# Hybrid attention and RWKV-7 block: block inverses made beside the chain of the unit ahead, q, k, v projections moved to the front

## The chip, the cores and the metric

The kernel runs on one core of a Trainium2 chip. The metric is device time in microseconds (us), the median of repeated executions. The engines are TensorE (PE in the rows, its weight loads PEld), VectorE (DVE), ScalarE (ACT), GpSimd (POOL) and SyncE (SP), which issues the DMAs.

## What is computed

One layer of a hybrid decoder block on 1024 positions of 1024 channels, in float32:

```python
u = rmsnorm(h, norm1_gain)
proj = u @ w_in
q, k, v, r_p, k_p, v_p, w_p, a_p, g_p, gate_a, gate_b = jnp.split(proj, split_at, axis=-1)
y_attn = sliding_window_attention(q, k, v, ...) @ w_branch_attn      # 8 blocks of 128 queries
y_rwkv = rwkv7_time_mix(r_p, k_p, v_p, w_p, a_p, g_p, ...) @ w_branch_rwkv
mixed = jax.nn.sigmoid(gate_a) * y_attn + jax.nn.sigmoid(gate_b) * y_rwkv
h = h + mixed @ w_out
hidden = jnp.square(jax.nn.relu(rmsnorm(h, norm2_gain) @ w_ff_in))
return h + hidden @ w_ff_out
```

The time mixing is a recurrence over positions, for each of 8 heads:

```python
def step(S, inp):
    r_t, w_t, k_t, v_t, a_t, b_t = inp
    sa = jnp.einsum('bhij,bhj->bhi', S, a_t)
    S = S * w_t[:, :, None, :] + sa[..., None] * b_t[:, :, None, :] + v_t[..., None] * k_t[:, :, None, :]
    return S, jnp.einsum('bhij,bhj->bhi', S, r_t)
```

## The kernel before

Every float32 matmul of the projections is made of three matmuls of split operands (a high and a low part), 128 by 128 weights by 512 columns. A projection of 128 output channels is 48 of them (`proj`, line 169, tile `ps_m`), or is part of a Strassen product (`group`, line 233, tile `psw`).

The program goes through these stages:

1. **Front.** The norm (`norm1`), two projections, then two branch gates (`gate`, tile `gt`). Meanwhile `in_sums` makes the seven right sides of the Strassen products, on DVE, ACT and POOL. `in_groups` then makes 16 of the projections in four groups (`GROUPS`), among them four gates.
2. **Phase 1.** The SBUF pools of the front are closed and others opened in their place, so phase 1 starts when the groups are through. It projects and prepares k, v and q (`prep_k`, `prep_v`, `prep_q`, `prep_rq`), and then works through eight *units*: one of four pairs of heads (p), one half of the sequence (hf). A unit has three parts:
   - `unit_e` (E): decays, keys and the 64 by 64 score blocks of the unit. Two pairs of score products `ps_s` (tag `s`, two buffers) are masked by DVE into `SA` and `SR` (line 673; two buffers of each). Parts of `SA` go to DRAM and come back as `LT`. Then DVE inverts 16 by 16 blocks in 15 steps of a product and a sum (lines 710 and 711), and the result goes out to `lx_d`.
   - `unit_m` (M): the inverse comes back as `XT`. From it PE, DVE and ACT make 64 by 64 inverses, in four rounds of small matmuls (`ps_z`, `ps_x`, with `ps_g` ahead of them; `XD` and `DZ` are DVE's transposes).
   - `unit_c` (C), *the chain*: eight chunks of 64 positions, one after the other. In each the state gives `ry` (PE), DVE adds it to `G0`, PE makes `pu`, DVE copies it to `UV` (line 788, eight in a chain), PE makes `pd`, and DVE the next state `sbd`. Behind the last chunk PE makes `py` from `UV` and `SR`, DVE adds it to `Yt`, normalises it, and writes `y` (line 830).
   
   Attention blocks (`attn_block`), the output gate of the time mixing (`prep_g`) and eight branch gates fill in by the table `PLAN`: one entry ahead of the units, one behind each unit.
3. **Branch stage.** Attention and time mixing are loaded as `yh`, `yl`, two last gates are made, then the branch projections, `w_out` and the MLP, as before and after alike.

A scheduler decides the order of each engine from priorities: `tc.high_priority(offset=...)` moves work forward by so many instructions (`HP_E` for E, `HP_C` for M and C). Each engine then works through its own list in order. A tile is taken when its buffer is free, so tags and buffer numbers also set the order. `M` and `C` share the tag `c` of PSUM (one buffer); `py` and the transposes behind it have the tag `y` (one buffer).

Of the kernel before, what the change touches and what calls it, by code (L numbers as in the profile page):

```python
# [60 lines left out]
def hybrid_block(ctx, tc, x_ap, xt_ap, win_ap, wst_ap, lora_ap, wbr_ap, wout_ap, wff1_ap, wff2_ap, cst_ap,  # L61
# [306 lines left out]
    wst = ExitStack()  # L368
    wp = wst.enter_context(tc.tile_pool(name="wspool", bufs=1))
    for i in range(2):  # L370
        gate(i)
    B_in = in_sums(wp)
    pqt.close()
    pw = [None, wst.enter_context(tc.tile_pool(name="pw1", bufs=1, space=PSUM, side="right"))]
    pst.close()
    pw[0] = wst.enter_context(tc.tile_pool(name="pw0", bufs=1, space=PSUM))
    pw.reverse()
    in_groups(wp, pw, B_in)
    wst.close()
    psum_pools(1)  # L380

# [5 lines left out]
    def phase1():  # L387
        st = ExitStack()
        lp = st.enter_context(tc.tile_pool(name="lpool", bufs=1))
        rp = st.enter_context(tc.tile_pool(name="rpool", bufs=1))  # L390
        ep = st.enter_context(tc.tile_pool(name="epool", bufs=1))
        ap = st.enter_context(tc.tile_pool(name="apool", bufs=1))

        cst[1] = lp.tile([P, CTOT - CKEEP], F32, name="cst1")
        nc.sync.dma_start(out=cst[1], in_=cst_ap[:, CKEEP:])
        smask = lp.tile([P, HALF], F32, name="smask")
        G.memset(smask, 1.0)
        G.memset(smask[:, ::64], 0.0)
# [15 lines left out]

        g0, g1, full = slice(0, 64), slice(64, 128), slice(0, 128)

        def prep_k():
            w = load_w(win_ap[2])
            for hf in range(2):
# [7 lines left out]
                rk = newton(ep, pk, 8, 1.0 / 64, RMS_EPS)  # L427
                rkx = ep.tile([P, 8, 64], F32, tag="e0", bufs=2, name="rkx")
# [23 lines left out]
        def prep_q(j):  # L452
            w = load_w(win_ap[4 + j])
            for hf in range(2):
# [4 lines left out]
                split_out(ps, [P, HALF], *(("k", "kkn") if hf else ("cum", "Wi")),  # L459
# [255 lines left out]
        def unit_m(p, hf, X):  # L715
            SA, UV, un = X["SA"], X["UV"], X["un"]
            G0 = rp.tile([P, 4, 128], F32, tag="G0", name="G0", bufs=1)
            half_ = [slice(0, 64), slice(64, 128)]
            ps = pp.tile([P, 4, 2, 64], F32, tag="c", name="ps_g", bufs=1)
# [17 lines left out]
            ps = pp.tile([P, 8, 64], F32, tag="c", name="ps_z", bufs=1)  # L737
# [4 lines left out]
            ps = pp.tile([P, 8, 64], F32, tag="c", name="ps_x", bufs=1)  # L742
# [10 lines left out]
            ps = pp.tile([P, 8, 32], F32, tag="c", name="ps_z", bufs=1)  # L753
# [5 lines left out]
            ps = pp.tile([P, 8, 32], F32, tag="c", name="ps_x", bufs=1)  # L759
# [87 lines left out]
        cnt = {"q": 0, "a": 0, "x": 6}  # L847

        def fill(steps):
            for c in steps.split():  # L850
# [470 lines left out]
```

## Time and profile before

| | |
|---|---|
| median of 3 runs | 1637.86 us (1637.47 to 1639.15) |
| profiled execution: its time, its span | 1639.25 us, 1637.4 us |
| PE, PEld busy | 1529.0 us (93%), 1209.8 us (74%) |
| DVE, ACT, POOL busy | 1116.4 us (68%), 661.8 us (40%), 205.2 us (13%) |
| mean granted clock of TensorE | 0.945 |

The span runs from the first to the last instruction. A busy PE is not PE at its peak, since its instructions overlap; the number of matmuls in a stretch and the granted clock tell more. A clock of 1.00 is 2.4 GHz, one of 0.50 is 1.2 GHz.

### The profile page before, as it was taken

What the parts mean: (1) busy time and instruction counts of PE and PEld (TensorE: products, weight loads), DVE (VectorE), ACT (ScalarE), POOL (GpSimd) and SP (SyncE); (2) the same over time, 40 slices, a digit from 0 to 9 for tenths busy, and PEclk for the clock granted to TensorE, in tenths of its full rate; (3) what the DMA queues carried; (4) which work ended last, traced back from release to release, by engine and by line L of the source; (5) the groups of instructions that cost most, each with busy time, mean ns of one, the idle gap of its engine ahead of it and who ended that gap; (6) DMA issues with size and microseconds to landing.
All of it is one profiled execution on the core that took longest, in us unless ns stands there. A gap on an engine that the chain in (4) does not pass through costs nothing.

```text
span 1637.4 us, 22102 instructions
## 1 busy us (share of the span) xinstructions
PE 1529.0 (93%) x8300; PEld 1209.8 (74%) x8300; DVE 1116.4 (68%) x2120; ACT 661.8 (40%) x1130; POOL 205.2 (13%) x124
## 2 busy tenths in 40 slices
PE   5999999878888999999399999999999999999998
PEld 5788877756666777777188888787878787878786
DVE  5944433258778898886556566959595959595958
ACT  6422342256455555655212434433243333333332
POOL 2100000000000000000000011231413232423220
PEclk9999998957778999998599999999999999999999
DMA  5223236424123332231543411111111111111112
GB/s 197 89 103 116 90 124 170 120 76 146 47 79 103 106 116 81 73 101 63 205 135 116 173 46 39 52 52 54 58 57 52 52 52 52 52 52 52 52 52 103
DMA packets 97466, 145.64 MB, mean 89 GB/s; under 512 B 26192, under 2 KB 48592, under 8 KB 97360
## 3 DMA queue, kind: packets, MB, share of 16 engines
q1 hardware_dynamic: 97360, 144.23, 26.5%
q8 instruction: 66, 1.08, 0.3%
q14 instruction: 40, 0.33, 0.1%
HBM read 108.54 MB, written 35.65 MB: 88 GB/s over the span
## 4 chain that ended last, share of the span: by engine, by line
PE 35%; DVE 12%; ACT 2%; issue 2%; DMA 1%; ACTq 0%; DVEq 0%
PE psy L233 14%; PE psx L233 11%; PE ps_m L169 9%; DVE wlo L226 3%; DVE c L1128 2%; DVE c L1108 2%; DVE tlo L1139 2%; PE ps_o L1049 1%; DVE h L1201 1%; ACT c L1111 1%; ACT whi L225 1%; DVE c L1176 1%; DVE c L1172 1%; DMA gg<-g_d 0%; DMA yt<-ya_d 0%
## 5 line engine op out<-in xcount | busy, mean ns | idle before, releaser
L233 PE MATMUL psy<-T,whi 128*128 128x512 f32 x512 | 159.6, 393 | 0.0
L169 PE MATMUL ps_m<-uh,wlo 128*128 128x512 f32 x320 | 134.1, 419 | 2.5 <-DVE wlo L162 2.5
L169 PE MATMUL ps_m<-ul,whi 128*128 128x512 f32 x320 | 133.7, 418 | 0.0
L169 PE MATMUL ps_m<-uh,whi 128*128 128x512 f32 x320 | 132.4, 414 | 0.0
L233 PEld LDWEIGHTS psy<-T,whi 128*128 128x128 f32 x512 | 96.1, 188 | 21.9
L233 PE MATMUL psx<-tlo,whi 128*128 128x512 f32 x256 | 101.9, 398 | 4.5 <-DVE tlo L1139 4.5
L226 DVE TENSOR_TENSOR wlo<-fraw_a,whi 128x1024 fp32r<-128x1024 f32 x47 | 65.0, 1383 | 59.6 <-ACT whi L225 59.6
L233 PE MATMUL psx<-thi,wlo 128*128 128x512 f32 x256 | 101.6, 398 | 1.5 <-DVE h L1201 0.9
L225 ACT CAST whi<-fraw_a 128x1024 fp32r<-128x1024 f32 x47 | 49.3, 1049 | 129.0 <-PE psy L233 85.6
L233 PE MATMUL psx<-thi,whi 128*128 128x512 f32 x256 | 101.1, 395 | 0.0
L233 PE MATMUL psy<-T,wlo 128*128 128x512 f32 x256 | 100.7, 393 | 0.0
L1201 DVE TENSOR_TENSOR h<-h,psx 128x1024 f32<-128x1024 f32 (+1 forms) x66 | 76.9, 1182 | 11.7 <-PE psx L233 11.7
L233 PE MATMUL psy<-tlo,whi 128*128 128x512 f32 x192 | 77.2, 402 | 3.1 <-DVE tlo L1139 3.1
L233 PE MATMUL psw<-T,whi 128*128 128x512 f32 x256 | 79.0, 390 | 0.0
L1081 POOL TENSOR_TENSOR fraw_a<-fraw_a,fraw_a 128x1024 f32<-128x1024 f32 x16 | 43.9, 2741 | 257.4 <-DVE s L1057 256.2
L233 PE MATMUL psy<-thi,wlo 128*128 128x512 f32 x192 | 75.9, 395 | 0.0
L233 PE MATMUL psy<-thi,whi 128*128 128x512 f32 x192 | 75.8, 395 | 0.0
L233 PE MATMUL psy<-B,whi 128*128 128x512 f32 x240 | 74.8, 392 | 0.0
L169 PEld LDWEIGHTS ps_m<-uh,wlo 128*128 128x128 f32 x320 | 61.9, 194 | 13.9 <-DVE wlo L162 2.9
L1138 ACT CAST thi<-c 128x1024 fp32r<-128x1024 f32 x56 | 58.7, 1048 | 32.2 <-DVE c L1128 31.9
L169 PEld LDWEIGHTS ps_m<-uh,whi 128*128 128x128 f32 x320 | 61.9, 193 | 11.7 <-issue 0.2
L169 PEld LDWEIGHTS ps_m<-ul,whi 128*128 128x128 f32 x320 | 62.0, 194 | 11.1 <-issue 0.9
(326 smaller groups left out, 3803.4 us busy)
## 6 DMA issues: line engine op xcount, KB each, us to landing
fraw_a<-wff SPq DMA_DIRECT2D x32, 512.0 KB, 3.2
wraw<-wff SPq DMA_DIRECT2D x32, 512.0 KB, 3.2
wraw<-win SPq DMA_DIRECT2D x40, 256.0 KB, 3.2
a<-wst SPq DMA_DIRECT2D x16, 512.0 KB, 3.3
gate_d<-gt SPq DMA_DIRECT2D x24, 256.0 KB, 2.0
z_d<-cw SPq DMA_DIRECT2D x22, 256.0 KB, 2.1
xt<-x SPq DMA_DIRECT2D x8, 512.0 KB, 5.8
la<-wa_d SPq DMA_DIRECT2D x8, 512.0 KB, 4.7
```

Of the source, the lines that this page charges most:

```text
L169: PE.matmul(out=out, lhsT=a, rhs=b, start=(n == 0), stop=(n == last))
L225: A.copy(out=hi, in_=src)
L226: V.tensor_sub(out=lo, in0=src, in1=hi.bitcast(F32))
L233: PE.matmul(out=out, lhsT=a, rhs=b, start=start and n == 0, stop=n == last, skip_group_check=True)
L1049: PE.matmul(out=pss[j], lhsT=a, rhs=b[:, sl], start=(k == 0 and n == 0), stop=(k == NK - 1 and n == 2))
L1081: G.tensor_sub(out=a21, in0=a11, in1=a21)
L1108: V.scalar_tensor_tensor(out=c, in0=c, scalar=0.0, in1=r2[:, (lo_, hi_)[hf]].unsqueeze(1).broadcast_to([P, 2, HALF]), op0=ALU.max, op1=ALU ...
L1111: A.activation(out=c, in_=c, func=AF.Square)
L1128: V.tensor_sub(out=C[out], in0=C[a], in1=C[out])
L1138: A.copy(out=hi, in_=src)
L1139: V.tensor_sub(out=lo, in0=src, in1=hi.bitcast(F32))
L1201: V.tensor_add(out=ht, in0=ht, in1=ps[:, c0 % 2:c0 % 2 + step])
```

## The change

- k, v and q are projected and prepared in the front, from a pool of their own (`qpool`): k and v ahead of `in_sums`, q ahead of `in_groups`. The two gates that stood there move into phase 1, and the fourth group makes gates 0 to 3 instead of 2 to 5.
- M of a unit is issued right behind its E, with E's priority, and ahead of C of the unit before. `G0` gets a second buffer, and the five PSUM tiles of M take the tag `y` instead of `c`.
- `HP_C` rises from 3000 to 3800.
- `PLAN` has a gate ahead of the units, and an attention block and a gate behind each. These are tied to the chain: a block may not be issued before a given chunk's `pu` of that unit (`issue_after`).

```diff
-HP_C = 3000
+HP_C = 3800
-PLAN = ("k v q q q q", "g", "a", "a", "a a", "a x", "a x", "a x", "a x x x x x")
+PLAN = ("g x", "a x", "a x", "a x", "a x", "a x", "a x", "a x", "a x x")
-GROUPS = ((9, 10, 1, 11), (12, 13, 14, 15), (16, 17, 18, 19), (22, 23, 24, 25))
+GROUPS = ((9, 10, 1, 11), (12, 13, 14, 15), (16, 17, 18, 19), (20, 21, 22, 23))
-    for i in range(2):
-        gate(i)
-    B_in = in_sums(wp)
+    def preps(qp):
...
+        prep_k()
+        prep_v()
+        yield
+        for j in range(4):
+            prep_q(j)
+        prep_rq()
+        yield
...
         def unit_m(p, hf, X):
-            G0 = rp.tile([P, 4, 128], F32, tag="G0", name="G0", bufs=1)
+            G0 = rp.tile([P, 4, 128], F32, tag="G0", name="G0", bufs=2)
-            ps = pp.tile([P, 4, 2, 64], F32, tag="c", name="ps_g", bufs=1)
+            ps = pp.tile([P, 4, 2, 64], F32, tag="y", name="ps_g", bufs=1)
...
-            ps = pp.tile([P, 8, 64], F32, tag="c", name="ps_z", bufs=1)
+            ps = pp.tile([P, 8, 64], F32, tag="y", name="ps_z", bufs=1)
...
         def unit_c(p, hf, X):
+            marks = []
             for c in range(8):
...
+                marks.append(last)
...
+        def mstage(n):
+            with tc.high_priority(offset=HP_E):
+                unit_m(n // 2, n % 2, xs[n])
+        cnt = {"a": 0, "x": 4}
+        def fill(steps, marks=None):
+            steps = steps.split()
+            for m, c in enumerate(steps):
+                with tc.issue_after(marks[8 * m // len(steps)]) if marks else nullcontext():
...
         prep_wa()
+        estage(0)
+        mstage(0)
         fill(PLAN[0])
-        estage(0)
         for n in range(8):
-            p, hf = n // 2, n % 2
-            with tc.high_priority(offset=HP_C):
-                unit_m(p, hf, xs[n])
             if n + 1 < 8:
                 estage(n + 1)
+                mstage(n + 1)
             with tc.high_priority(offset=HP_C):
-                unit_c(p, hf, xs[n])
-            fill(PLAN[n + 1])
+                unit_c(n // 2, n % 2, xs[n])
+            fill(PLAN[n + 1], xs[n]["marks"])
...
+    qp = wst.enter_context(tc.tile_pool(name="qpool", bufs=1))
+    todo = preps(qp)
+    next(todo)
+    B_in = in_sums(wp)
+    next(todo)
```

What the scheduler makes of it is shown at three places. In the names below the number behind a tile tells one unit's from another's.

The first place is PE's list where a chain ends, before. `pu_4001` and `py_4011` belong to unit 2, `ps_g_4223` is M of unit 3 and `ps_s_4417` is E of unit 4.

```order
L175 MATMUL pu_4001<-G0_3615,XT_3634 64x64 x2
L175 MATMUL py_4011<-UV_3147,SR_3150 64x64 x10
L791 MATMUL pd_4005<-UV_3147,BKt_3148 128x128
L175 MATMUL py_4011<-UV_3147,SR_3150 64x64 x6
L169 MATMUL ps_m_7017<-uh4_145,whi_6981 128x512
L169 MATMUL ps_m_7017<-uh5_146,wlo_6982 128x512
L781 MATMUL ry_4519<-sbd0_1659,AR_3725 128x128
L724 MATMUL ps_g_4223<-UV_3727,SA_3729 64x64 x16
```

In the change, `py_3677` is that of unit 1 (it reads `SR_2637`, a buffer that unit 3 takes next), `pu_4255` is the second `pu` of the chain of unit 2, and `ps_s_4046` and `ps_s_4047` are the second pair of score products of unit 3.

```order
L175 MATMUL py_3677<-UV_2634,SR_2637 64x64 x16
L799 MATMUL pd_4247<-UV_3284,BKt_3285 128x128
L788 MATMUL ry_4251<-sbd1_2140,AR_3282 128x128
L175 MATMUL ps_s_4046<-AR_3955,BK_3956 128x128
L175 MATMUL pu_4255<-G0_3462,XT_3481 64x64 x2
L175 MATMUL ps_s_4047<-AR_3955,BK_3956 128x128
```

`py` of a unit stood behind its own last `pu` and ahead of the next M. It now stands behind the whole M of the next unit and the first `pu` of the next chain, and the second pair of `ps_s` stands behind it, inside that chain.

The second place is DVE's list around the first `UV` of a chain. Before, `UV_5802` is the first of the chain of unit 6, and `SA_6482` and `SR_6483` are unit 7's:

```order
L673 TENSOR_TENSOR SA_6482<-ps_s_6569,cst1_1650 128x4x64
L149 SCALAR_TENSOR_TENSOR nw_6113<-nw_6113 128x8
L673 TENSOR_TENSOR SR_6483<-ps_s_6569,cst1_1650 128x4x64
...
L673 TENSOR_TENSOR SA_6482<-ps_s_6570,cst1_1650 128x4x64
...
L710 TENSOR_TENSOR LT_6583<-LT_6583 128x2
L711 TENSOR_REDUCE LT_6583<-LT_6583 128x1
L788 COPY UV_5802<-pu_6658 64x128
```

In the change, `UV_3957` is the chain of unit 3, `SA_4642`, `SR_4643` and `LT_4745` are unit 4's, `Yt_4240` is unit 2's:

```order
L679 TENSOR_TENSOR SA_4642<-ps_s_4717,cst1_2132 128x4x64
L679 TENSOR_TENSOR SA_4642<-ps_s_4718,cst1_2132 128x4x64
...
L796 COPY UV_3957<-pu_4931 64x128
L817 TENSOR_TENSOR Yt_4240<-Yt_4240,py_4349 128x512
...
L679 TENSOR_TENSOR SR_4643<-ps_s_4717,cst1_2132 128x4x64
...
L679 TENSOR_TENSOR SA_4642<-ps_s_4731,cst1_2132 128x4x64
...
L796 COPY UV_3957<-pu_4959 64x128
L148 TENSOR_TENSOR nw_4375<-nw_4375 128x8
L679 TENSOR_TENSOR SA_4642<-ps_s_4732,cst1_2132 128x4x64
...
L716 TENSOR_TENSOR LT_4745<-LT_4745 128x2
```

All masks of the next unit stood ahead of the chain's first `UV`. Now the first pair of `SA` does, and `SR` and the second pair stand behind it: the last `SA` behind the third `UV`, and the first step of the inversion behind the fifth.

The third place is PE's list in the front of the change: `ps_m_620` and `ps_m_658` are the two halves of v, `pt_526` are the transposes of k's first half, and `pk_573` the head sums of its second.

```order
L169 MATMUL ps_m_620<-uh7_148,wlo_613 128x512
L404 MATMUL pt_526<-cst_83,rkx_524 128x128 x4
L169 MATMUL ps_m_620<-ul7_156,whi_612 128x512
L169 MATMUL ps_m_620<-uh7_148,whi_612 128x512
L370 MATMUL pk_573<-cst_83,sq_571 128x2 x4
L169 MATMUL ps_m_658<-uh0_141,wlo_613 128x512
```

Gates stood at this place before. The transposes wait for `rkx`, which DVE makes in the midst of its list for `in_sums`, behind 33 of its 40 operations.

## Rows read from the trace of the kernel before

**Rows 1.** Busy us of each engine by stretch, instructions, granted clock, DMA share, GB/s

```profile
40.00:80.00 40.00, 37.08 (x152) 29.39 (x151) 39.43 (x50) 16.73 (x28) 9.09 (x6) 0.96 0.27 98
80.00:235.00 155.00, 155.00 (x676) 126.67 (x676) 62.29 (x54) 48.72 (x54) 0.53 (x3) 1.00 0.27 100
235.00:320.00 85.00, 77.90 (x357) 62.11 (x355) 23.81 (x61) 23.75 (x43) 1.81 (x10) 0.94 0.55 153
320.00:413.00 93.00, 73.02 (x454) 54.37 (x455) 65.31 (x247) 51.80 (x125) 0.87 (x8) 0.67 0.38 117
459.00:521.00 62.00, 54.16 (x447) 41.34 (x446) 50.42 (x185) 36.12 (x83) 1.38 (x8) 0.82 0.32 97
663.00:711.00 48.00, 47.51 (x442) 35.70 (x441) 41.44 (x155) 28.26 (x72) 0.77 (x3) 1.00 0.29 89
```

**Rows 2.** Timeline of DVE and POOL in the front: start us, length us

```profile
39.69 9.94 DVE L247 TENSOR_TENSOR s<-uh,ul 128x512 f32<-128x512 f32 x6
49.56 1.28 DVE L162 TENSOR_TENSOR wlo<-wraw,whi 128x512 fp32r<-128x512 f32 x2
38.06 11.03 POOL L242 TENSOR_TENSOR e<-uh,ul 128x512 f32<-128x512 f32 x7
```

**Rows 3.** Timeline of SP's queue where phase 1 opens, and the page's DMA landings

```profile
235.70 0.43 SPq L553 DMA_DIRECT2D z<-lz_d  x1
247.50 0.62 SPq L608 DMA_DIRECT2D la<-wa_d  x1
la<-wa_d SPq DMA_DIRECT2D x8, 512.0 KB, 4.7
```

**Rows 4.** Timeline of PE and DVE, unit 0 from its first product to its chain

```profile
319.48 0.50 PE L175 MATMUL ps_l<-la,lwl 64*128 64x512 f32 x1
350.59 0.42 DVE L673 TENSOR_TENSOR SA<-ps_s,cst 128x256 f32<-128x256 f32 x1
391.73 0.29 DVE L711 TENSOR_REDUCE LT<-LT 128x8 f32<-128x128 f32 x1
413.38 0.28 DVE L788 COPY UV<-pu 64x128 f32<-64x128 f32 x1
```

**Rows 5.** Groups of lines, the inversion's two: busy us, mean ns

```profile
L710 DVE TENSOR_TENSOR LT<-LT 128x2 f32<-128x2 f32 (+14 forms) x120 | 32.0, 266 | 1.3
L711 DVE TENSOR_REDUCE LT<-LT 128x1 f32<-128x2 f32 (+14 forms) x120 | 26.1, 218 | 1.5
```

**Rows 6.** Timeline of DVE, from the masks of unit 6 to the chain of unit 7

```profile
657.47 0.42 DVE L673 TENSOR_TENSOR SA<-ps_s,cst 128x256 f32<-128x256 f32 x1
662.95 0.28 DVE L788 COPY UV<-pu 64x128 f32<-64x128 f32 x1 [0.86 <-PE pu L175]
702.03 0.42 DVE L673 TENSOR_TENSOR SA<-ps_s,cst 128x256 f32<-128x256 f32 x1
710.14 0.16 DVE L710 TENSOR_TENSOR LT<-LT 128x2 f32<-128x2 f32 x1
711.03 0.28 DVE L788 COPY UV<-pu 64x128 f32<-64x128 f32 x1 [0.54 <-PE pu L175]
729.28 0.29 DVE L711 TENSOR_REDUCE LT<-LT 128x8 f32<-128x128 f32 x1
735.36 0.29 DVE L788 COPY UV<-pu 64x128 f32<-64x128 f32 x1
751.58 0.28 DVE L788 COPY UV<-pu 64x128 f32<-64x128 f32 x1 [1.37 <-PE pu L175]
```

**Rows 7.** Timeline of PE behind the last chunk of unit 5

```profile
689.57 1.36 PE L175 MATMUL py<-UV,SR 128*64 128x64 f32 x32
```

**Rows 8.** Timeline of DVE, end of phase 1

```profile
788.93 0.69 DVE L830 TENSOR_TENSOR y<-y,bv 128x512 f32<-128x512 f32 x1 [2.32 <-ACT y L828]
```

**Rows 9.** Timeline of DVE, first and last `UV` of the chain of unit 1

```profile
459.35 0.28 DVE L788 COPY UV<-pu 64x128 f32<-64x128 f32 x1 [1.15 <-PE pu L175]
488.72 0.29 DVE L788 COPY UV<-pu 64x128 f32<-64x128 f32 x1
```

More of the change, by code (lines that the diff above doesn't have):

```diff
@@ L466, in prep_rq, with phase1, half, split_out @@
         def prep_rq():
-            a = newton(ep, rqs.rearrange("p a b c -> p (a b c)"), 64, 1.0 / 64, RMS_EPS,
-                       buf=half(F32, "Wi", "nwq"))
+            a = newton(qp, rqs.rearrange("p a b c -> p (a b c)"), 64, 1.0 / 64, RMS_EPS,
+                       buf=half(F32, "r", "nwq"))
             V.tensor_scalar(out=rq, in0=a, scalar1=0.125, scalar2=None, op0=ALU.mult)
+        prep_k()
[5 more added lines that the diff above has]
+        yield
+    def phase1():
+        st = ExitStack()
+        lp = st.enter_context(tc.tile_pool(name="lpool", bufs=1))
+        rp = st.enter_context(tc.tile_pool(name="rpool", bufs=1))
+        ep = st.enter_context(tc.tile_pool(name="epool", bufs=1))
+        ap = st.enter_context(tc.tile_pool(name="apool", bufs=1))
+        cst[1] = lp.tile([P, CTOT - CKEEP], F32, name="cst1")
+        nc.sync.dma_start(out=cst[1], in_=cst_ap[:, CKEEP:])
+        smask = lp.tile([P, HALF], F32, name="smask")
+        G.memset(smask, 1.0)
+        G.memset(smask[:, ::64], 0.0)
+        amk = ap.tile([P, 256], F32, name="amk")
+        nc.sync.dma_start(out=amk, in_=amk_ap)
+        def half(dt, tag, name):
+            return ep.tile([P, HALF], dt, tag=tag, name=name, bufs=2 if tag == "e0" else 1)
+        def split_out(src, shape, t0, t1, dsts):
+            hi = ep.tile(shape, F32R, tag=t0, name="sp_h")
+            lo = ep.tile(shape, F32R, tag=t1, name="sp_l")
+            A.copy(out=hi, in_=src)
+            V.tensor_sub(out=lo, in0=src, in1=hi.bitcast(F32))
+            for part, rows, dst in dsts:
+                nc.sync.dma_start(out=dst, in_=(lo if part else hi)[rows].bitcast(F32))
         def attn_in(b):
@@ L845, in estage @@
                 unit_e(p, hf, lws[p], xs[n])
[L847 to L866 removed]
+        def mstage(n):
[6 more added lines that the diff above has]
+                with tc.issue_after(marks[8 * m // len(steps)]) if marks else nullcontext():
+                    if c == "g":
+                        prep_g()
+                    elif c == "a":
+                        attn_block(cnt[c])
+                    else:
+                        gate(cnt[c])
+                if c != "g":
+                    cnt[c] += 1
         prep_wa()
+        estage(0)
+        mstage(0)
         fill(PLAN[0])
[L870 removed]
         for n in range(8):
[L872 to L874 removed]
             if n + 1 < 8:
                 estage(n + 1)
+                mstage(n + 1)
             with tc.high_priority(offset=HP_C):
[L878 to L879 removed]
+                unit_c(n // 2, n % 2, xs[n])
+            fill(PLAN[n + 1], xs[n]["marks"])
         st.close()
+    wst = ExitStack()
+    wp = wst.enter_context(tc.tile_pool(name="wspool", bufs=1))
+    qp = wst.enter_context(tc.tile_pool(name="qpool", bufs=1))
[3 more added lines that the diff above has]
+    next(todo)
+    pqt.close()
+    pw = [None, wst.enter_context(tc.tile_pool(name="pw1", bufs=1, space=PSUM, side="right"))]
+    pst.close()
+    pw[0] = wst.enter_context(tc.tile_pool(name="pw0", bufs=1, space=PSUM))
+    pw.reverse()
+    in_groups(wp, pw, B_in)
+    wst.close()
+    psum_pools(1)
     phase1()
```

66 lines of the change are left out of this document (14 added, 52 removed).

## The prediction

> **What bounds the kernel now.** I read the kernel by stages, since PE's 93% is a mean over stages with different limits. In the front PE has its fill: 676 matmuls in 155 us, 0.229 us each at clock 1.00 [rows 1]. The 848 us behind phase 1 are as full, and the change does not touch them. Phase 1 is different. From 320 to 413 us there are 454 matmuls in 93 us at clock 0.67, and nothing but the first unit's E and M ends that stretch. Later, from 663 to 711, DVE is busy 41.44 of 48 us [rows 1].
>
> So I looked at what sets the time from one chain to the next, which I call the period, by the first `UV` of each. Unit 6's last mask of `SA` starts at 657.47, 5.5 us ahead of the first `UV` of chain 5 at 662.95. Its own chain starts at 711.03, 53.1 us after that mask ended. For unit 7 it is 702.03 and 751.58, or 49.1 us [rows 6]. In those 50 us lie the trip of `SA` through DRAM (702.45 to 710.14, 7.7 us), the inversion, which shares DVE with the chain ahead (710.14 to 729.57, 19.4 us), and the way of the result through DRAM and M (729.57 to 751.58, 22.0 us; 21.4 us for unit 0, from 392.02 to 413.38 [rows 4]). A period of some 48 us is these 50 us, less the few us by which the masks run ahead of the chain in front.
>
> **The change, part by part.** The sum is made in places along the trace, against the profiled execution's 1639.25 us (1637.4 of span and 1.85 around it), 1.4 us above the median.
>
> *Front.* The stage from 235 to 320 that made k, v and q (85 us [rows 1]) goes ahead of the groups. The two gates leave: 96 matmuls at 0.229, or 22 us. That they covered `in_sums` brings nothing back: the stall at 40 to 50 us comes from a weight's split that stands behind six additions of 1.66 us each on DVE [rows 2], and k's weight takes the same place. Of the 85 us, 288 matmuls are 66, and 19 are head sums, transposes and stalls. In the new place PE waits for `rkx` behind `in_sums`, which keeps DVE busy 39.4 of 40 us [rows 1], so I leave the 19. Phase 1 opens 85 - 22 = 63 us later, at 298 (bounds: 54 and 72, with half of the 19 gone or half as much again).
>
> *Up to the first chain.* Unit 0's E needs the small projection shifted, sent out and back: the load of `z` is issued at 235.70, that of `la` at 247.50, and `la` lands 4.7 us on [rows 3], 17.2 us after the opening. That was hidden behind k, v, q; now only one gate lies beside it. The first product, at 319.48 before [rows 4], comes at 298 + 17 = 315. From there to the chain it took 93.9 us, with two attention blocks and unit 1 in DVE's list between. These now come later, so I take less. To the last mask 24 us (31.5 in the rows, and I leave about a quarter for the neighbours). Through DRAM 7.7. The inversion 9: its rows follow each other now, and the floor is 32.0 + 26.1 over eight units, 7.3 [rows 5]. M 21.4. That is 62 us (bounds 50 and 94). Chain 0 starts at 377.6 instead of 413.38: **35.8 us won**.
>
> *Chain 0 to chain 1.* Unit 1's masks now stand about at the first `UV` of chain 0, so chain 1 follows by the mean of 53.1 and 49.1, 51 us, against 46.0 (413.38 to 459.35 [rows 4, 9]): **5 us lost**.
>
> *The six periods from chain 1 to chain 7.* Before, they took 292.2 us (459.35 to 751.58 [rows 6, 9]). M now holds PSUM's one buffer `y` from `ps_g` to its last product, and it is ahead of the older unit's `py`. So `py`, 1.36 us [rows 7], waits for all of M and stands behind the next chain's first `pu`. `SR` of the unit after next needs the buffer that this `py` reads, its second pair of score products needs the PSUM buffers that `SR` has to empty, and the second half of `SA` follows from these. What is queued behind is the inversion. The loop is then: M ends, chain n starts, `py`, `SR`, second `SA`, DRAM, inversion, DRAM, M of unit n+1. The masks, once 5.5 us ahead of the chain in front, end behind its third `UV`: two chunks of 3.48 us (711.03 to 735.36 over seven [rows 6]), 1.4 for `py` in the first, and the masks, 9.5 us in all. From there to the next chain I take 47.5 us, less than 49.1, since the inversion is stretched over three chunks and no longer seven: 17 instead of 19.4. The bounds are 44 (an inversion of 14) and 53. One period is 57.0, six are 342: **49.8 us lost**. Work moved here (two gates, 22 us of PE) I cost at nothing: in a period of 57 us PE has room, and what this costs at a low clock is rival B.
>
> *End.* From the first `UV` of chain 7 to the end of `y` it was 751.58 to 789.62, 38.0 us [rows 6, 8]. Attention's last block and two late gates now lie beside it, and they fill an idle PE. I leave 38.0.
>
> The sum: -35.8 + 5.0 + 49.8 = +19.0 us, with the last `y` at 808.6 and not 789.6. 1639.25 + 19.0 - 1.4 = **1657 us**. The sign turns at a period of 57.0 - 19.0 / 6 = 53.8 us.
>
> **Rivals.**
>
> *A: DVE is the bound, the loop hides* (faster). M runs beside the chain ahead as the words of the change have it, and a period falls to what DVE has to do: 41.44 us busy of 48 [rows 1], say 45. Six of them are 270, and the sum is -35.8 + 5.0 - 22.2 = -53, so 1585. For it: DVE is the busiest engine of the stage. Against it: the order puts the second masks behind the chain's third `UV`, and 9.5 us and the 44 us at least that must follow don't fit into 45. The Trainium skill (Perfetto Trace Analysis, Identifying the Most-Contended Engine) would read it so: for VectorE, occupancy is a fair measure of how close an engine is to its roofline. By that rule alone the time is this rival's; the trace agrees that DVE's share is high (86%), and no run here shows yet whether it still leads when a loop is longer than DVE's work. Chance 0.12.
>
> *B: the loop as forecast, at a low clock* (slower still). The granted clock was 0.82 from 459 to 521 and 1.00 from 663 to 711 [rows 1]. The later stretch is the denser one (442 matmuls in 48 us against 447 in 62). The change spreads the gates, one to a longer period. A chain took 29.4 us in the first stretch (459.35 to 488.72 [rows 9]) and 24.3 in the second [rows 6]. With half to all of these 5 us in seven periods it is +17 to +35: 1674 to 1692, middle 1680. The Trainium skill (TensorE: Matmul & The Clock Gate, Part 1) states that the default state is throttled and that activity releases the throttle; the rows agree, in that the emptier stretches stand at 0.67 and 0.82. Chance 0.18.
>
> *C: gain and loss cancel.* Period 54, from an inversion that finishes in 14 us: six are 324, the sum +1, 1639. For it: less of attention's work competes in a longer period. Against it: the way through DRAM and M took over 21 us in both units read. Chance 0.12.
>
> **How the numbers follow.** The forecast keeps 0.58. It spreads over 1640 to 1675 by its bounds (first chain 10 us either way, 3 us a period). The range over the cases is 1622 to 1692: it takes in C, B and the forecast's tails, and leaves out A. I count 0.2%, some 3.3 us, as what a measurement can tell from no change. Faster: all of A, 0.05 of C and 0.05 of the forecast's lower tail, 0.22. Same: 0.05 of C and 0.03 of the forecast, 0.08. Slower: the rest, 0.70.
>
> **What would show it.** In the trace of the change: phase 1 opening near 298 (52 or more us beyond 235); the first `UV` near 378, then steps of 51 and 57; the last mask of a unit some 9 us behind the first `UV` of the chain ahead; `py` right behind the first `pu` of the next chain; DVE with idle time in each period, some 41 us busy of 57; last `y` near 809. I am wrong if the period is under 53.8, above all if the 47.5 us from mask to chain shrink because DVE has fewer neighbours, or if the opening comes much earlier. A stretch of 0.5 clock through most periods with steps of 60 and more is rival B.

## The result and the profile after

The changed kernel takes 1696.56 us in the median (1694.2 to 1698.18) against 1637.66 us for the kernel before. The ratio is 1.0358 [1.034, 1.0375], 59 us slower. The prediction said 1657 us with a range up to 1692: the direction and the mechanism were right, the size was not, and the time lies above the range. The profiled execution took 1694.2 us, its span is 1692.4 us, 55.0 us above that of before.

The stretches of the changed kernel: start and end, length, busy us of PE, PEld, DVE, ACT and POOL with the number of instructions, granted clock, DMA share, GB/s.

```profile
140.00:298.00 158.00, 157.04 (x688) 128.07 (x686) 64.84 (x67) 48.03 (x53) 0.00 (x0) 1.00 0.28 97
298.00:387.00 89.00, 50.91 (x351) 38.40 (x351) 49.10 (x125) 34.75 (x61) 3.08 (x19) 0.69 0.46 146
442.00:503.40 61.40, 53.69 (x415) 40.29 (x417) 44.85 (x163) 28.76 (x73) 1.26 (x7) 0.75 0.26 77
442.00:798.00 356.00, 308.93 (x2518) 237.84 (x2518) 263.66 (x952) 175.62 (x445) 5.02 (x24) 0.80 0.24 71
798.00:838.80 40.80, 37.79 (x251) 29.93 (x252) 29.48 (x110) 21.78 (x60) 0.00 (x0) 0.87 0.08 27
```

Phase 1 opens at 298 us, as forecast, and the stretch up to the first chain is shorter than before. The six periods from chain 1 to chain 7 are the fourth line: 356.0 us, where before they were 292.2 [rows 6, 9]. No engine fills them: DVE is busy 263.66 of 356.0 us (74%), PE 308.93 (87%) with about as many matmuls as before (2518 against 2560), and the clock fell from 0.96 to 0.80.

One period on DVE, rows that answer to [rows 6] (start us, length us, and in brackets the wait ahead of it):

```profile
442.01 0.28 DVE L796 COPY UV<-pu 64x128 f32<-64x128 f32 x1 [4.19 <-PE pu L175]
444.43 0.69 DVE L817 TENSOR_TENSOR Yt<-Yt,py 128x512 f32<-128x512 f32 x1 [2.14 <-PE py L175]
446.57 0.42 DVE L679 TENSOR_TENSOR SR<-ps_s,cst 128x256 f32<-128x256 f32 x1
448.70 0.29 DVE L796 COPY UV<-pu 64x128 f32<-64x128 f32 x1 [0.32 <-PE pu L175]
453.51 0.28 DVE L796 COPY UV<-pu 64x128 f32<-64x128 f32 x1 [0.29 <-PE pu L175]
453.79 0.41 DVE L679 TENSOR_TENSOR SA<-ps_s,cst 128x256 f32<-128x256 f32 x1
464.77 0.16 DVE L716 TENSOR_TENSOR LT<-LT 128x2 f32<-128x2 f32 x1
482.27 0.28 DVE L717 TENSOR_REDUCE LT<-LT 128x8 f32<-128x128 f32 x1
503.37 0.28 DVE L796 COPY UV<-pu 64x128 f32<-64x128 f32 x1 [0.79 <-PE pu L175]
```

Read it as a ring. Chain 1 starts (442.01); the `Yt` addition that follows belongs to unit 0, whose chain ended at 418.6; only then `SR` of unit 2 is written (446.57), its last `SA` follows 9.4 us behind that addition (453.79), the inversion runs from 464.77 to 482.55, and chain 2 starts 20.8 us later (503.37). PE, at the end of the same period, shows why `Yt` is late:

```profile
491.31 1.91 PE L746 MATMUL ps_z<-XD,SA 64*64 64x64 f32 x32
501.03 1.07 PE L768 MATMUL ps_x<-XT,DZ 32*32 32x32 f32 x32 [0.21 <-ACT DZ L764]
502.64 0.69 PE L175 MATMUL pu<-G,XT 64*64 64x64 f32 x4
503.26 1.97 PE L175 MATMUL py<-UV,SR 128*64 128x64 f32 x32
505.16 0.80 PE L799 MATMUL pd<-UV,BKt 128*128 128x128 f32 x2
```

`py` of unit 1 stands behind the last product of unit 2's M and the first `pu` of chain 2, and ahead of that chain's `pd`. It takes 1.97 us, not the 1.36 of [rows 7].

### The profile page after: what moved, and what is told of

Read it like the earlier page. It is cut to its first block, busy times and chain, and to the rows that moved or that the text cites. A ratio compares the mean times of both kernels' runs of the same rounds, so it can differ in the third digit from the quotient of the medians.

```text
span 1692.4 us, 22067 instructions
## 1 busy us (share of the span) xinstructions
PE 1555.0 (92%) x8300; PEld 1237.0 (73%) x8300; DVE 1126.3 (67%) x2120; ACT 664.0 (39%) x1130; POOL 204.0 (12%) x124
## 4 chain that ended last, share of the span: by engine, by line
PE 65%; DVE 22%; ACT 5%; DMA 4%; issue 3%; SPq 1%; DVEq 0%; ACTq 0%; POOL 0%; POOLq 0%
PE ps_m L169 16%; PE psy L233 13%; PE psx L233 11%; PE psw L233 9%; DVE wlo L226 3%; DVE c L1150 2%; DVE c L1130 2%; DVE tlo L1161 2%; PE po L169 2%; PE pu L175 1%; PE ps_o L1071 1%; DVE h L1223 1%; PE pd L799 1%; ACT c L1133 1%; PE pk L370 1%
## 5 line engine op out<-in xcount | busy, mean ns | idle before, releaser
L169 PEld LDWEIGHTS ps_m<-ul,whi 128*128 128x128 f32 x320 | 63.0, 197 | 11.6
```

Source lines behind the costliest of these rows:

```text
L169: PE.matmul(out=out, lhsT=a, rhs=b, start=(n == 0), stop=(n == last))
```

## The experiments

Each edit is one to the changed kernel unless it says otherwise. The first column of places is the first `UV` of chain 0, the next the six periods from chain 1 to chain 7 with their clock, then the end of the last `y` and of attention's last product `po`. The branch stage begins, with `yh`, 6 to 10 us behind the later of these two (in E1 and E7 1 to 2 us ahead of it). The time is the median of all executions, the places are those of the profiled one, which took 1668.67 us in E1 and 1641.78 in E5, 10 above and 7 below their medians.

| run | what | median us | ratio to before | chain 0 | six periods, clock | `y`, `po` end |
|---|---|---|---|---|---|---|
| | before | 1637.66 | 1 | 413.4 | 292.2, 0.96 | 789.6, 775.6 |
| | after | 1696.56 | 1.0358 [1.034, 1.0375] | 387.1 | 356.0, 0.80 | 838.8, 840.5 |
| E1 | three `SR` | 1658.87 | 1.0154 [1.012, 1.0189] | 386.9 | 325.1, 0.82 | 805.6, 820.0 |
| E2 | `py`, `pt` in tag `t` | 1730.73 | 1.0588 [1.0568, 1.0609] | 386.1 | 358.2, 0.79 | 849.5, 876.2 |
| E3 | nothing tied | 1680.59 | 1.0278 [1.026, 1.0296] | 389.6 | 353.4, 0.86 | 833.8, 774.3 |
| E4 | `HP_C` 3000 | 1689.24 | 1.0327 [1.0304, 1.035] | 387.3 | 352.5, 0.81 | 834.1, 835.7 |
| E5 | front alone | 1649.12 | 1.0086 [1.005, 1.0122] | 392.2 | 300.8, 0.94 | 791.7, 792.0 |
| E6 | M beside the chain alone | 1689.32 | 1.0328 [1.0309, 1.0348] | 409.9 | 358.6, 0.87 | 840.1, 745.7 |
| E7 | three `SR`, three `AR` | 1677.01 | 1.0259 [1.024, 1.0278] | 382.0 | 314.7, 0.84 | 814.9, 829.3 |
| E8 | three `SR`, nothing tied | 1638.37 | 1.0016 [1.0001, 1.003] | 389.7 | 305.1, 0.94 | 789.4, 767.7 |
| E9 | M in tag `c` | 1835.30 | 1.1207 [1.1187, 1.1228] | 429.6 | 429.6, 0.69 | 974.9, 982.5 |
| E10 | E8, last blocks tied | 1662.88 | 1.016 [1.0144, 1.0175] | 388.8 | 325.2, 0.78 | 806.6, 808.2 |
| E11 | E5, last blocks tied | 1660.45 | 1.015 [1.0132, 1.0167] | 393.3 | 308.7, 0.80 | 796.9, 806.0 |
| E13 | `py` in tag `c` | 1672.11 | 1.0205 [1.0183, 1.0227] | 388.2 | 298.4, 0.87 | 780.9, 825.5 |
| E14 | E13, nothing tied | 1646.74 | 1.0061 [1.0048, 1.0075] | 387.4 | 285.6, 0.96 | 769.8, 796.3 |
| E15 | E14, `HP_C` 3000 | 1648.91 | 1.0071 [1.0056, 1.0086] | 388.4 | 274.8, 0.97 | 757.5, 801.8 |
| E16 | E15, attention ahead of gates | 1670.37 | 1.0204 [1.0189, 1.0219] | 401.6 | 304.2, 0.90 | 822.0, 712.2 |
| E17 | E5, attention ahead of gates | 1679.05 | 1.0259 [1.0242, 1.0275] | 404.9 | 309.6, 0.89 | 829.1, 698.1 |
| E18 | E16, gates tied | 1700.01 | 1.0381 [1.0364, 1.0398] | 403.5 | 319.4, 0.82 | 846.4, 786.9 |

E12 (E10 with M in tag `c`) took 1844.74 us, 1.1271 [1.1254, 1.1287].

The theory T1 was the prediction's loop: M, `py`, `SR`, masks, inversion, M. Its rivals were the blocks tied to the chain with the low clock that goes with them (T2), the front move (T3) and the chain's rank (T4).

### Which half of the change costs

E5 takes the changed kernel and undoes the second half: M in its own unit's turn and in tag `c`, the chain at 3000, nothing tied. The second copy of `G0` and the new `PLAN` stay.

```diff
-HP_C = 3800
+HP_C = 3000
...
         estage(0)
-        mstage(0)
...
+            with tc.high_priority(offset=HP_C):
+                unit_m(n // 2, n % 2, xs[n])
             if n + 1 < 8:
                 estage(n + 1)
-                mstage(n + 1)
...
-            fill(PLAN[n + 1], xs[n]["marks"])
+            fill(PLAN[n + 1])
```

> The q, k, v projections in front and the new plan alone: M goes back into its own unit's turn (behind the chain ahead), in PSUM tag c, the chain at priority 3000, nothing tied to a chain. T1 (the loss of the change is the loop that M beside the chain makes, the front move itself gains): first chain at about 386 instead of 413 us, periods as in the kernel before (46 to 54, mean 48.3 us), 1637 - 27 = 1610, with up to 20 us for two more gate blocks that must find a place: 1605 to 1630 us, faster than before. Rival T3 (with q, k, v gone from phase 1 its stages have less to run, the clock falls and the stages get longer): periods of 52 us and more, 1640 us or above.

E6 is the opposite, the kernel before with M beside the chain. The lines left out here give it `HP_C` 3800, two `G0` and tag `y` for M's tiles, as in the change:

```diff
...
+        with tc.high_priority(offset=HP_E):
+            unit_m(0, 0, xs[0])
...
                 estage(n + 1)
+                with tc.high_priority(offset=HP_E):
+                    unit_m((n + 1) // 2, (n + 1) % 2, xs[n + 1])
...
```

> The kernel before with M beside the chain alone: M at E's priority ahead of the chain of the unit ahead, PSUM tag y, two G0, the chain at 3800; q, k, v stay in phase 1 and nothing is tied. T1: the same loop through SR and tag y, so 7 periods of 57 to 60 us against 48.3: 1637 + 7 x 9 to 11 = 1700 to 1715 us. T3: the loss sits in the front move, so this one is within 10 us of before, 1627 to 1650 us.

E6 alone loses 52 of the 59 us, with the six periods as long as in the whole change (358.6 against 356.0). That is less than the 1700 us and more that T1 expected: its first period, 29.8 us and not 46.0, gave 16 us back. T3 is out as the main cause. But T1's hope for E5 failed too: the front move reaches chain 0 21 us earlier and still ends up 12 us slower in the median (its five executions lie between 1641.8 and 1658.4 us). In the profiled one the 21 us are lost again step by step: chain 0 to chain 1 grew by 7.9 us (46.0 to 53.8), the six periods by 8.6, and the end from the first `UV` of chain 7 to `y` by 6.8 (38.0 to 44.8). Before, TensorE was already busy 280.76 of 292.25 us in the six periods.

### Is it the loop through SR and y?

E1 gives the buffer that the loop needs:

```diff
-            SR = rp.tile([P, 2, 8, 64], F32, tag="SR", name="SR", bufs=2)
+            SR = rp.tile([P, 2, 8, 64], F32, tag="SR", name="SR", bufs=3)
```

> The second mask buffer SR of the changed kernel gets a third copy (bufs=3), nothing else. Theory T1 (a loop through buffers): in the changed kernel the SR of unit n+2 waits for py of unit n, py waits in PSUM tag y for all of M of unit n+1, so the last SA mask of unit n+2 falls 12 to 16 us behind the first UV of a chain, and the inversion, M and the next chain behind it: period 59.3 us. With three SR the masks and the inversion no longer wait for py, and a period is set by the 44 to 46 us of VectorE work in it: about 48 to 50 us, 7 periods x 9 to 11 = 63 to 77 us less, about 1620 to 1635 us. The inversion should begin before the first UV of the chain ahead. Rival T2 (attention and gates tied to the chain leave TensorE empty, its clock low, and that is what makes a period long): the SR copies change at most 1 or 2 us a period, 1680 to 1697 us.

DVE in E1, the same period as above, and the last mask of the next unit:

```profile
427.28 0.41 DVE L679 TENSOR_TENSOR SA<-ps_s,cst 128x256 f32<-128x256 f32 x1
436.30 0.16 DVE L716 TENSOR_TENSOR LT<-LT 128x2 f32<-128x2 f32 x1 [0.28 <-POOL LT L695]
439.17 0.28 DVE L796 COPY UV<-pu 64x128 f32<-64x128 f32 x1 [1.48 <-PE pu L175]
466.68 0.29 DVE L717 TENSOR_REDUCE LT<-LT 128x8 f32<-128x128 f32 x1
490.71 0.28 DVE L796 COPY UV<-pu 64x128 f32<-64x128 f32 x1
496.48 0.41 DVE L679 TENSOR_TENSOR SA<-ps_s,cst 128x256 f32<-128x256 f32 x1
```

The last mask of unit 2 moved from 11.8 us behind the first `UV` of chain 1 to 11.9 us ahead of it, and the inversion begins before the chain. Units 4, 6 and 7 also have their masks ahead (3.3 to 11.6 us); those of units 3 and 5 still come 5.8 and 5.3 us behind (490.71 and 496.48 for unit 3). So that is the mechanism, but only half the size: 38 us of the 63 to 77 expected. The inversion of unit 2, 17.8 us in the changed kernel, takes 30.7 here, beside a whole chain on DVE; over units 2 to 7 the mean went from 16.7 to 26.6. The way from unit 2's last mask to its chain grew from 49.6 to 63.4 us.

E2 and E9 were to take `py` out of tag `y` or M out of it.

```diff
-            py = pp.tile([P, 4, 2, 64], F32, tag="y", name="py", bufs=1)
+            py = pp.tile([P, 4, 2, 64], F32, tag="t", name="py", bufs=1)
```

> py and pt of the chain take PSUM tag t instead of y, so that tag y holds M's five tiles alone; SR stays at two buffers. T1: py is no longer behind M, comes right behind its own chain, some 25 us earlier than now, SR comes free with it, and the loop of 59.3 us falls to 48 to 50 us: 1620 to 1640 us, near the run with three SR. If the first is faster and this one is not, the SR buffer matters but not by way of tag y. T2: no change beyond 5 us, 1687 to 1700 us. The attention's pt_t shares tag t, which could give back a few us.

```diff
-            ps = pp.tile([P, 4, 2, 64], F32, tag="y", name="ps_g", bufs=1)
+            ps = pp.tile([P, 4, 2, 64], F32, tag="c", name="ps_g", bufs=1)
...
```

> The changed kernel with M's five PSUM tiles back in tag c; SR stays at two buffers, the blocks stay tied. The run with py in tag t did not free py: it waited there for the attention and came 35 to 42 us behind its chain. Here nothing but py and pt uses tag y. T1 (the order M, py, SR, masks is the loop): the Yt addition comes 1 to 3 us behind the last UV of its chain instead of 27 us, the last SA mask no longer 8 to 10 us behind that addition but before or near the next chain's first UV, and the time falls as with three SR: 1650 to 1670 us. Rival (M and the chain now wait for each other in the single buffer of tag c): 1685 us or more with chains of 36 us and longer.

Both expectations failed, and in a way that teaches. In E2 `py` waited for the attention that uses tag `t`; DVE shows unit 2's `Yt` 36 us behind its chain:

```profile
514.47 0.30 DVE L796 COPY UV<-pu 64x128 f32<-64x128 f32 x1
550.32 0.69 DVE L817 TENSOR_TENSOR Yt<-Yt,py 128x512 f32<-128x512 f32 x1 [1.27 <-PE py L175]
552.01 0.41 DVE L679 TENSOR_TENSOR SR<-ps_s,cst 128x256 f32<-128x256 f32 x1
560.09 0.41 DVE L679 TENSOR_TENSOR SA<-ps_s,cst 128x256 f32<-128x256 f32 x1
```

The last mask follows `Yt` by 9.8 us (9.4 above), so the loop answers to the dose. Unit 0's `Yt` came 21 us ahead of chain 1's first `UV`, and the period behind it is 42.3 us. Unit 1's came 4 us behind that of chain 2, and the period is 61.2. The next four came 7.5 us behind, and the periods are 60.2 to 65.2 us.

In E9 T1's first signs held: `Yt` came 1.0 to 1.8 us behind its chain, and the last masks ahead of the next chain. But M of a unit and the chain ahead share one buffer, and M comes first, as the rival had it. So the first `pu` of chain 1 stands behind the last product of unit 2's M:

```profile
505.70 1.06 PE L768 MATMUL ps_x<-XT,DZ 32*32 32x32 f32 x32 [0.83 <-ACT DZ L764]
507.60 0.69 PE L175 MATMUL pu<-G,XT 64*64 64x64 f32 x4 [0.84 <-ACT XT L770]
```

A chain waits for all of the next unit's E and M, 76 to 82 us a period; the last chain, which has no next unit, follows in 32.6. E12 repeats that with three `SR`.

> Three SR, M in tag c, nothing tied but the last blocks. T1: with three SR the tag no longer matters for the loop, so within 6 us of the run with three SR and M in tag y. If M and the chain get in each other's way in tag c: 8 us or more above it.

It came out 182 us above E10, which differs from it in the tag alone: tag `c` is in the way whatever the copies of `SR`.

What E2 and E9 have in common is that a buffer of a tag goes round in the order of the code. That is also why `py` had to wait for M in the change: `mstage(n + 1)` is written ahead of `unit_c(n)`. The place that the code order leaves for `py` is tag `c`, behind its own chain's last `pd` and ahead of the next `pu`. E13:

```diff
-            py = pp.tile([P, 4, 2, 64], F32, tag="y", name="py", bufs=1)
+            py = pp.tile([P, 4, 2, 64], F32, tag="c", name="py", bufs=1)
```

> The changed kernel with py alone in PSUM tag c (pt stays in y with M's tiles, SR has two buffers, the blocks stay tied). In the runs so far a single buffer of a tag went round in the order of the code: M of unit n+1 stands ahead of chain n in the code, so py in y waits for M, and with M in c the chain waited for all of M (79 us a period). In c py comes behind the last pd of its own chain and ahead of the next chain's pu. T1: the Yt addition falls 1 to 3 us behind its chain's last UV instead of 25 to 29 us, SR is free with it, the last SA mask comes before the next chain's first UV, and the run is within 10 us of the one with three SR, 1650 to 1668 us; the first chunk of a chain, no longer behind py, takes 4 instead of 6 us. If T1 is wrong (SR was only in the way because three buffers also moved other work), 1680 us or more.

```profile
486.90 0.28 DVE L796 COPY UV<-pu 64x128 f32<-64x128 f32 x1 [1.24 <-PE pu L175]
489.91 0.43 DVE L679 TENSOR_TENSOR SA<-ps_s,cst 128x256 f32<-128x256 f32 x1
514.12 0.29 DVE L796 COPY UV<-pu 64x128 f32<-64x128 f32 x1
517.85 0.69 DVE L817 TENSOR_TENSOR Yt<-Yt,py 128x512 f32<-128x512 f32 x1
527.93 0.41 DVE L679 TENSOR_TENSOR SA<-ps_s,cst 128x256 f32<-128x256 f32 x1
541.45 0.15 DVE L716 TENSOR_TENSOR LT<-LT 128x2 f32<-128x2 f32 x1
544.36 0.28 DVE L796 COPY UV<-pu 64x128 f32<-64x128 f32 x1 [0.58 <-PE pu L175]
```

Unit 2's `Yt` comes 3.7 us behind its last `UV` (514.12), unit 4's last mask 16.4 us ahead of chain 3 (544.36), the first chunk of that chain takes 4.6 us, and six periods are 298.4 us, 57.6 less than in the changed kernel with two `SR` as before. With E1 that shows the loop and both its links, the buffer of `SR` and tag `y`. Not every unit profits alike: units 2, 4 and 6 have their last mask 11 to 16 us ahead of the chain in front, units 3, 5 and 7 still 2 to 5 us behind its first `UV` (486.90 and 489.91 for unit 3), and the periods go with it: 44.6, 57.5, 42.0, 60.3, 44.7 and 49.4. The time fell by only 24.5 us and lies 4 us above T1's range, because now attention, tied to the chains, ends last (825.5 against 780.9 for `y`).

E7 asked whether `AR`, the next buffer with two copies that a chain reads to its end, holds E1's periods at 54 us.

```diff
...
-            v2 = ap.tile([P, 2, 2, 128], F32R, tag="av", name="av", bufs=2)
+            v2 = ap.tile([P, 2, 2, 128], F32R, tag="av", name="av", bufs=1)
...
-            AR = rp.tile([P, 4, 4, 64], F32, tag="AR", name="AR", bufs=2)
+            AR = rp.tile([P, 4, 4, 64], F32, tag="AR", name="AR", bufs=3)
...
```

> The changed kernel with three SR and three AR (room made by one copy of av and of the gate's gt instead of two). In the run with three SR the first SA mask of unit n+2 came 7 to 12 us behind the last UV of chain n for n = 1, 2, 3, 4, 5, as if AR (two buffers, read by the chain to its last chunk) were the next buffer of the loop. T1b: with three AR the mask no longer follows the chain's end, a period falls from 54 to 47 to 49 us: 1659 - 6 x 5 to 7 = 1617 to 1630 us. Rival T5 (VectorE, shared by the inversion, the chain and the attention, is the limit): the period stays at 52 to 55 us, 1650 to 1668 us.

It doesn't: the first mask of unit n+2 still follows the last `UV` of chain n by 8 to 11 us (n = 1 to 5), and the six periods are 52.4 us each, where T5 put them. `wc` also has two copies and is read by the chain's last `sbd`. The trace points at it: DVE writes the `wc` of unit n+2 0.1 to 0.3 us behind that `sbd` (n = 1 to 5; 0.2 to 0.7 us in the kernel before). A third copy was not tried, so what holds the periods there is not shown. Unit 1's E came 27 us later than in E1 (first mask 408.0 against 380.6). One copy of `av` and `gt` instead of two may be the reason; it stays open, so E7's time says little.

### Ties, rank and clock

E3 and E4 change one of these each:

```diff
-                with tc.issue_after(marks[8 * m // len(steps)]) if marks else nullcontext():
+                with tc.issue_after(marks[8 * m // len(steps)]) if False else nullcontext():
```

> The attention and gate blocks are no longer tied to the chain (no issue_after), their places in the priority order stay. T1: the loop through SR and tag y stays, 59 us a period, time within 10 us of the changed kernel (1686 to 1706 us). T2: the blocks fill the stretch in front of a chain again, the granted clock there rises from 0.75 towards the 0.84 and more of the front, a period falls to about 50 us and the time to about 1640 us.

```diff
-HP_C = 3800
+HP_C = 3000
```

> The chain's priority offset goes back from 3800 to 3000, the rest is the changed kernel. T1: the order of waits through SR and py stays; within 10 us of the changed kernel. Rival T4 (the chain's higher priority is what pushes masks and inversion of the next unit back): the masks come 3 to 6 us earlier behind a first UV, six periods x 3 to 6 = 18 to 36 us less, 1660 to 1678 us.

E4 gained 7 us, inside what T1 allowed. E3 gained 16, more than the 10 that T1 allowed but not where T2 put it: the six periods stayed at 353.4 us although their clock rose to 0.86 (in E6 358.6 us at 0.87). E3's first four of them, and its last two:

```profile
438.70:668.80 230.10, 223.21 (x1916) 168.16 (x1918) 187.28 (x671) 129.26 (x323) 4.05 (x20) 0.99 0.34 104
668.80:792.10 123.30, 91.81 (x730) 71.48 (x728) 78.30 (x292) 50.29 (x135) 0.98 (x4) 0.61 0.10 27
```

With the clock at 0.99 a period is 57.5 us, at 0.61 it is 61.7; E6 has three of 57.6 us at 1.00 (510.35 to 683.10). So the loop doesn't come from the low clock, which adds some us to it. E3's gain lies in chain 1, 3 us earlier, in the six periods, another 3, and in what no longer spills, 7: 672 gate and branch matmuls behind `y` and not 801.

> Three SR and nothing tied to the chain. Alone the two gave 38 and 16 us. If they are apart (the loop, and a clock or a spill that ties cost), they add up: 1659 - 16 = 1643 us. If untying gained only by moving work around the same wait for SR, nothing is added: 1654 to 1665 us.

E8 joins E1 and E3. The two add up (38 + 16 = 54 us, measured 58), and the time is that of before. So these two make up the net loss: the loop, and the ties, 16 us with the loop and 20.5 without. The rest of the change is nothing in sum, but not part by part: against the kernel before, E8 is 23.7 us earlier at chain 0 and loses 5.3 us up to chain 1, 12.9 in the six periods and 5.2 in the end. E1 and E8 differ in the ties alone, and the six periods fall from 325.1 us at 0.82 to 305.1 at 0.94. How much of that is the clock stays open: untying moves work as well, and E1's profiled execution is 9.8 us above its median.

E10 and E11 put the last attention block and two gates back behind chain 7's marks, to fill an end that ran at a clock near 0.5.

```diff
-            fill(PLAN[n + 1], xs[n]["marks"])
+            fill(PLAN[n + 1], xs[n]["marks"] if n == 7 else None)
```

> Three SR, nothing tied but the last attention and two gate blocks, which are tied to chain 7. In the run with three SR and nothing tied TensorE was busy 94% of the periods, and the last 43 us, with nothing left to fill them, had a granted clock of 0.54. If TensorE's work and its clock now set the periods: two gates leave the periods (each some 15 us of TensorE over six periods, 3 to 4 us each) and lift the clock of the end, at a spill of up to 7 us: 1620 to 1633 us, faster than before. Rival (the two gates push the work behind phase 1 back one for one): 1636 to 1650 us.

> The front move alone, with the last attention and two gate blocks tied to chain 7. The front move alone gained 21 us up to the first chain and gave back 16 us in the periods (TensorE 97% busy there) and 7 us in the end at a clock of 0.50. If that is TensorE's work in the wrong place: 1649 - 10 to 20 = 1629 to 1639 us. If the periods are long for another reason: 1645 to 1657 us.

Both were worse than without, by 24 and 11 us, and lie above both of their ranges. The windows between the same chains, first E8's (chain 5 to chain 6), then E10's:

```profile
644.80:693.20 48.40, 45.23 (x436) 34.55 (x436) 44.15 (x162) 28.05 (x73) 0.72 (x2) 1.00 0.26 82
```

```profile
654.20:714.70 60.50, 49.14 (x361) 38.34 (x360) 42.05 (x159) 25.62 (x66) 0.72 (x2) 0.55 0.13 34
```

E10 has 75 matmuls fewer in this period, and its PE is busy longer, at a clock of 0.55: the period takes 12 us more. Less filler did not shorten this stretch; the clock fell with it.

### What is left when loop and ties are gone

> py in tag c and nothing tied. T1 and the clock: as three SR and nothing tied (1638 us), less the 2 us that py costs in the first chunk of each of seven chains: 1620 to 1635 us, faster than before. Rival T5 (the stage is then bound by TensorE at its clock and by VectorE, 50.9 us a period whatever the chain waits for): 1634 to 1645 us, no better than before.

> py in tag c, nothing tied, the chain's priority back at 3000 (alone on the changed kernel that gave 7 us). If the chain's higher rank only pushes the next unit's masks and inversion back: 5 to 10 us below the run with 3800. If the chain's order no longer matters: within 4 us of it.

E14 (E13 and E3 together) came out 2 us above its ranges, E15 (E14 and E4) within 4 us of E14. They have periods of 47.6 and 45.8 us, shorter than the 48.7 of before, and `y` ends 20 and 32 us earlier. Nothing of that reaches the time. Attention now ends last, at 796.3 and 801.8 us. DVE in E15, its last `y` and attention pieces around it:

```profile
756.76 0.69 DVE L839 TENSOR_TENSOR y<-y,bv 128x512 f32<-128x512 f32 x1
765.98 0.69 DVE L535 TENSOR_TENSOR pl<-pt_t,ph 128x512 fp32r<-128x512 f32 x1 [0.25 <-ACT ph L534]
773.11 0.69 DVE L535 TENSOR_TENSOR pl<-pt_t,ph 128x512 fp32r<-128x512 f32 x1
780.39 0.69 DVE L535 TENSOR_TENSOR pl<-pt_t,ph 128x512 fp32r<-128x512 f32 x1 [0.25 <-ACT ph L534]
```

A piece each 7.2 us, on engines that have little else: from 757 to 802 us PE is busy 25.37 of 45.0 us, at a clock of 0.50. So I ranked attention ahead of the gates:

```diff
-                        attn_block(cnt[c])
+                        with tc.high_priority(offset=300):
+                            attn_block(cnt[c])
```

> py in tag c, nothing tied, chain at 3000, and the attention blocks ranked ahead of the gates (priority offset 300). In the run without that rank the last unit's y stood at 757 us, 32 us earlier than in the kernel before, with periods of 46.4 us, but attention went on to 802 us, one piece each 7 us on an empty TensorE at a clock of 0.50, and from its end the rest took the same time as ever, about 844 us. Theory T6 (with the loop gone the attention's own pace is what ends phase 1): attention now ends before the last chain, phase 1 at 765 to 780 us, 1612 to 1630 us, faster than before. Rival T5 (VectorE and TensorE are full, attention in front only delays E and the chain): periods of 50 us, 1638 to 1655 us.

> The front move alone (M in its own turn) with the same rank for attention. There y (791.7 us) and the last attention piece (790 us) ended together, so the rank has nothing to shorten: 1640 to 1655 us. If the rank gains here as much as beside the chain, then M beside the chain is worth nothing and the rank everything: 1615 to 1632 us.

> As the first run of these three, with the gates (not the attention) tied to the chains, one to a chain. If gates must be spread so that TensorE's clock holds to the last chain: at or up to 10 us below the first run. If a tied gate leaves E and M on an empty TensorE at a low clock, as in the changed kernel: 10 to 30 us above it.

E16 and E17 missed both of their ranges, E16's T6 clearly. Attention in E16 ended at 712 us, but unit 1's E was pushed back (chain 1 at 478 us, 40 us later than in E15) and the last chains ran without filler (clock 0.71 from 680 to 780 us, `y` at 822). M beside the chain, with `py` in tag `c`, is worth 9 us against E17. E18, with gates tied, is 30 us above E16, at the edge of its second case; its six periods have a clock of 0.82 where E16's have 0.90.

## Why the prediction was wrong

The terms, as the prediction put them, against the trace after:

| term | predicted | measured |
|---|---|---|
| phase 1 opens | 298 | 298 |
| up to chain 0 | -35.8 (377.6) | -26.3 (387.1) |
| chain 0 to chain 1 | +5.0 | +8.9 |
| six periods | +49.8 (57.0 each) | +63.8 (59.3 each) |
| end, to the last `y` | 0 | +2.8 |
| behind the last `y` | 0 | +5.8 |
| sum | +19.0 | +55.0 |

All five terms missed the same way, by 36.0 us together.

**The loop: right, by E1, E2, E9 and E13.** It runs as described, through `py` in tag `y` and `SR`, and with the clock near 1.00 it takes the length forecast (57.5 and 57.6 us in E3 and E6, 57.0 forecast). The second part of its length, from the end of the last mask to the next chain, was forecast at 47.5 us, and the six measure 49.2, 49.2, 46.6, 47.0, 46.3 and 44.2, a mean of 47.1. In that there is luck: the pieces named for it, 7.7 us through DRAM, 17 of inversion and 22.0 for the way back and M, make 46.7, and they measured 10.2, 16.7 and 20.2 in the mean. The 7.7 us were the shortest of eight units (7.7 to 20.4).

**The step that failed is the size of the first part.** "Two chunks of 3.48 us, 1.4 for `py`, and the masks, 9.5 us in all" was 12.3 us in the mean (10.3 to 14.6), from the first `UV` to the end of the last mask. In the period shown the two chunks took 6.7 and 4.8 us (442.01, 448.70, 453.51): 3.48 came from a chain at clock 1.00, and this stretch stands at 0.50, `py` takes 1.97 us with `pd` behind it, and DVE's list puts `Yt`, its mean and two `SR` masks between the `UV`. The clock is the larger share: where these chunks ran at 1.00, four times each in E3 and E6, the first part was 10.3 and 10.5 us in the mean, and at 0.50, four times in the changed kernel, 12.9. Some 1 us of the miss is there at full clock too. (In E3 and E6 the work beside the loop differs as well, so this parting is rough.) 2.8 us, less the 0.4 of the second part, are the 14.0 us missed in six periods. A row's duration was carried from a full stretch to an empty one, and a part of the work that the new order puts there was left out.

**Up to chain 0** 9.5 us were missed. The first product came at 322.26 and not 315: the small projection's `z` was issued at 303.80, six us after the opening, behind other loads in SP's queue, where I had taken the opening itself. To the last mask it took 21.6 us and not 24, but the way through DRAM, the inversion and M 9.9, 9.9 and 23.5 us against 7.7, 9 and 21.4.

**Chain 0 to chain 1** took 54.9 us and not 51. Unit 1's last mask ended 0.6 us behind chain 0's first `UV`, as forecast, but its inversion, beside that chain on DVE, took 24.1 us.

**"Work moved here I cost at nothing"** failed in two places. In the changed kernel 129 gate matmuls spilled past the last `y`, tied to its chain, where before none did (801 against 672), and the way from `y` to the end took 5.8 us more; in E3, untied, both are gone (672 matmuls, 847.0 us). That the spill cost no more is due to room that the prediction had denied ("as full"), the first 36 us behind `y`, before and after:

```profile
789.60:826.00 36.40, 19.06 (x47) 11.69 (x48) 17.45 (x18) 8.99 (x9) 0.00 (x0) 0.60 0.70 245
838.80:875.00 36.20, 36.20 (x161) 29.35 (x160) 17.97 (x19) 13.89 (x19) 0.00 (x0) 1.00 0.84 276
```

And in E5, where no loop leaves room, the front move lost all of the 21 us that it won at chain 0 (7.9, 8.6 and 6.8).

**Rivals.** B (a low clock) is half right: the clock was 0.80 in the periods and lengthened the first chunks, but E3 and E6 have a loop of nearly the same length at 0.99 and 1.00. A, by DVE's share, fell: 74% busy in the changed kernel, and one more copy of `SR` took 31 us from the six periods with DVE's work about the same (263.66 and 252.06 us). Nor was DVE the busiest engine in the row that A used: TensorE was busy 47.51 of 48 us there. By the Trainium skill (Perfetto Trace Analysis, Identifying the Most-Contended Engine) a vector engine's occupancy is a fair measure of how near it is to its roofline; that agrees with these rows, since DVE was not near it and did not set the time. C needed a period of 54 with the loop in place, from an inversion of 14 us: the inversion took 14.2 to 19.3 us, and no period of the six was under 57.4.

The sign would have turned at a period of 53.8 us by the forecast's other terms, at 50.2 by the measured ones; the loop's 59.3 is longer than either.

## What to carry to other kernels

When a stage is moved ahead of another in the code, ask which single buffer the two now share, and who is behind it: buffers of a tag go round in code order, so a late user in the old unit can hold the next but one unit. A period longer than any engine's busy time can be such a ring; walk it once by the first and last instruction of each part, and take durations from a stretch with the clock and the neighbours that the new one will have. Then free one link of it at a time, as E1 and E13 did, and look at every unit, not at one. Freeing a ring gains only up to the next thing that ends last, here attention, which ended behind `y` in E14 and E15.

## What the runs showed that I had not expected

Fewer matmuls made TensorE busy for longer: 361 in 49.14 us at a granted clock of 0.55 (E10) against 436 in 45.23 us at 1.00 (E8), in the same place of the program. The Trainium skill (TensorE: Matmul & The Clock Gate, Part 1) has the throttled state as the default that activity releases; these two windows agree with it.

No version beat the kernel before. E8 is within 0.2% of it. Whether a plan exists that keeps E15's 45.8 us periods and also ends attention by 757 us stays open; the two tries with M beside the chain (E16 and E18) traded one for the other.
